# A second chunk of 128 tokens gathers its U rows, the dense U products become 256 wide, and more of them run ahead of the expert loop

## The chip, the cores and the metric

The kernel runs on one core of one Trainium2 chip. The metric is the device time of one execution in microseconds (us). A core has five engines with queues of their own: TensorE (PE in the profile; its weight loads are PEld), VectorE (DVE), ScalarE (ACT), GpSimd (POOL) and SyncE (SP), and 16 DMA engines which all of them feed. Here SP issues most loads, ACT most stores, and POOL the gathers, in which each partition fetches a row of its own.

## What is computed

One layer of an encoder on 512 tokens of width 1024: a layer norm, a projection, neighbourhood attention and latent attention, an output projection and a second layer norm; all of that is ahead of the part that changes. Then comes a feed-forward part with 16,384 experts, in which every token uses 128 (8 heads with 16 each):

```python
s1 = einsum('thd,kd->thk', q[..., :half], sub_keys[0]);  s2 = ...   # 128 keys each
v1, i1 = top_k(s1, 16);  v2, i2 = top_k(s2, 16)
cv, ci = top_k(v1[..., :, None] + v2[..., None, :], 16)              # over the 256 pairs
idx = e1 * 128 + e2                                                  # 128 experts a token
g = softmax(cv)
act = g * gelu(einsum('td,ted->te', xb, u_table[idx]))
out = einsum('te,ted->td', act, v_table[idx])
```

A sigmoid gate on a second input is added, and a last layer norm ends it.

## The kernel before

**Two ways to the experts.** Tokens come in four chunks of 128. For chunk 0 (`N_G = 128` tokens) the kernel gathers, for each of a token's 128 experts, the row of U and the row of V (4 KB each): one gather fetches 128 rows, one per token, 512 KB. VectorE multiplies such a tile with the tokens and sums along it (`gather_u`, line 1140), or adds it, scaled, to `base[0]` (`gather_v`, line 1149). For the other 384 tokens (`N_D`) the second product is dense: a matrix G, 16,384 experts by 384 tokens, holds each token's softmax weights and zeros elsewhere; it is built by one-hot products and kept in DRAM (`g_dram`, 24 parts of 16 tokens, 1 MB each). Experts come in 128 blocks of 128. The loop (line 1205) takes a block of G, multiplies it with the block's activations where these were computed densely, cuts it and the block's V rows into a high and a low part, and PE adds three products for each pair (`mm3`, line 103; `expert_out`, line 1163) into six PSUM banks, `acc`. That is 18 products 512 wide a block.

**The activations.** Of those 384 tokens the first `N_S = 96`, all in chunk 1, gather their U rows too: `own_rows` (line 885) fetches rows and multiplies them on VectorE with copies of the tokens (`h_s`), and the result is multiplied into the softmax weights `gws` before G is built from them. 96 tokens with 128 experts don't fill 128 partitions evenly, so the tokens are taken as groups of 64 and 32 (`S_PARTS`), and their index and result tables are moved between layouts by six small DMAs each way (`slices`, lines 892 to 911). There are 96 gathers. The last `N_U = 288` tokens get their activations densely, from products of each U block with all 288 tokens. `LEAD = 73` of the 128 blocks are done ahead of the loop, as plain f32 products (`lead_block`, line 942: 8 matmuls 288 wide, no cutting). The other 55 are done in the loop with `mm3` (`expert_in`, line 630): 24 products 288 wide, after ACT and VectorE have cut the block (`split`, line 86). The first `SPILL = 56` of the blocks ahead are stored to DRAM (`ge_dram`) and come back in the last part of the loop (line 1231).

**The stages around the change.** After the scores (lines 693 to 716) come, in an order written by hand for all engines (lines 1074 to 1100): `route` for chunk 1 (which experts, which weights), then `route` and `build_g` for chunk 2, the same for chunk 3, `route` for chunk 0, and last `build_g` for chunk 1, whose weights have to wait for its own rows. `run` (line 1056) goes through their steps. Each step yields an estimate of its VectorE time; `run` puts PE work beside it, `PACE = 1.1` us for each estimated us, taken from `gate_and_leads` (line 1012): the gate's products and the U blocks. With a share given (`OWN = 0.98`), it also puts in steps of `own_rows`, so many us of rows for one us of other steps. Nothing of `own_rows` is left for the last build. What PE work is left after it stands in the passage to the loop (lines 1183 to 1201), between the last product of G, the first load of G from DRAM (on POOL's queue, line 1187) and the first cut of V.

**Gathers of chunk 0.** They are 128 steps with U, one activation, and 128 with V. `PRE = 14` steps are done in the passage; the loop spreads the others by a formula (lines 1247 to 1252): an iteration counts 1 while U blocks are left in it, and `LATE = 0.5` after that, so that gathers run dense in the first part and half as dense in the second. They end some six iterations before the loop. `GATS = 8` buffers let POOL run ahead of VectorE.

Of the kernel before, what the change touches and what calls it, by code (L numbers as in the profile page):

```python
# [9 lines left out]
F32 = mybir.dt.float32  # L10
# [9 lines left out]
D = 1024  # L20
# [22 lines left out]
PRE = 14  # L43
OWN = 0.98
OWN_LATE = 10.0
# [8 lines left out]
NO_GATHER = 1  # L54
GE_AHEAD = 12
LOW = -3.0e38
FEED_NA = 2.75
# [8 lines left out]
def tile_encoder_layer(ctx: ExitStack, tc: tile.TileContext, A: dict, out: bass.AP):  # L66
# [559 lines left out]
    g_sel = pB.tile([128, NGC, 128], F32, name="g_sel")  # L626
    i_sel = pB.tile([128, NGC, 128], I32, name="i_sel")
    ge_t = {}

    def expert_in(i):  # L630

        ps = psH.tile([128, 512], F32, name="hp")
        u = stream(A["uT"][i], [8, 128])
        for k in range(8):
            mm3(ps[:, :N_U], (u[0][:, k], u[1][:, k]), (hTh[:, k, ts], hTl[:, k, ts]), k == 0, k == 7)
        ge = pB.tile([128, N_U], F32, name="ge", bufs=LEAD - SPILL + 1)
        nc.scalar.activation(ge, ps[:, :N_U], AF.Gelu)
        if i < SPILL:
            nc.sync.dma_start(ge_dram[i], ge)
        else:  # L640
            ge_t[i] = ge
# [174 lines left out]
    def build_g(c, e1, e2, gw, first):  # L816
# [64 lines left out]
        leave(ahead[0], sums)  # L881

    def own_rows(e1, e2, gw):
        ix = rg.tile([N_S, 128], I32, name="s_ix")
        nc.vector.scalar_tensor_tensor(ix, e1[0:N_S], 128.0, e2[0:N_S], op0=OP.mult, op1=OP.add)
        sel = rg.tile([128, N_S], I32, name="s_sel")
        dots = rg.tile([128, N_S], F32, name="s_dot")
        act = rg.tile([N_S, 128], F32, name="s_act")  # L890

        def slices():

            for lo, hi in S_PARTS:
                n = hi - lo
                for j in range(128 // n):
                    yield (slice(j * n, (j + 1) * n), slice(lo, hi)), (slice(lo, hi), slice(j * n, (j + 1) * n))

        for there, here in slices():
            nc.gpsimd.dma_start(sel[there], ix[here])  # L900
        yield 0.4
        for (lo, hi), x in zip(S_PARTS, h_s):
            for k in range(lo, hi):
                u = wst.tile([128, D], F32, name=("whi", "wlo")[k % 2])
                nc.gpsimd.indirect_dma_start(out=u[:], out_offset=None, in_=u_rows,
                                             in_offset=bass.IndirectOffsetOnAxis(ap=sel[:, k:k + 1], axis=0))
                nc.vector.scalar_tensor_tensor(u, u, 1.0, x, op0=OP.mult, op1=OP.mult, accum_out=dots[:, k:k + 1])
                yield 1.17
# [4 lines left out]
        nc.vector.tensor_tensor(gw[0:N_S], gw[0:N_S], act, op=OP.mult)  # L913

# [17 lines left out]
    def leave_u(i, ps):  # L932
        ge = pB.tile([128, N_U], F32, name="ge", bufs=LEAD - SPILL + 1)
# [140 lines left out]
    with tc.manual_schedule(engines={nc.vector.engine, nc.scalar.engine, nc.tensor.engine, nc.sync.engine,  # L1074
# [23 lines left out]
        run(lead0)  # L1098
        run(build)
        pb.close()  # L1100
# [29 lines left out]
    acc = [[psA.tile([128, 512], F32, name=f"acc{c}{hf}") for hf in range(2)] for c in range(NDC)]  # L1130
    hdot = pG.tile([128, NGC, 128], F32, name="hdot")
    scr = pG.tile([128, D], F32, name="scr")
# [70 lines left out]
    with tc.manual_schedule(engines={nc.vector.engine, nc.sync.engine}):  # L1203
        expert_in(LEAD)
        for n, i in enumerate(order):
# [23 lines left out]
            if 0 <= n + GE_AHEAD - (128 - SPILL) < SPILL:  # L1229
                ge = pB.tile([128, N_U], F32, name="ge", bufs=LEAD - SPILL + 1)  # L1230
                nc.sync.dma_start(ge, ge_dram[order[n + GE_AHEAD]])
# [126 lines left out]
```

## Time and profile before

| what | us |
|---|---|
| median of 3 runs | 1576.03 |
| lowest and highest | 1575.24, 1579.82 |
| the profiled execution, its own time | 1581.24 |
| its span | 1579.5 |

The profiled execution is a single run, 5.2 us above the median. In the profile an idle time is put down to what ended it; `<-` in a group stands between what an instruction writes and what it reads; "x128" is a count. An f32 matmul leaves two records each on PE. Records of matmuls overlap, since they are pipelined, so a matmul's cost is read from the distance between starts and not from a record's length.

| group of instructions | count | busy us |
|---|---|---|
| DVE products of chunk 0's U rows (L1142) | 128 | 156.6 |
| DVE sums of chunk 0's V rows (L1153) | 128 | 163.9 |
| PE records of U blocks ahead of the loop (L952, in `mm` and `hp`) | 624 and 544 | 157.5 and 137.1 |
| DVE cuts of 128x1024 blocks, U's among them (L90, `wlo`) | 134 | 157.1 |

### The profile page before, as it was taken

What the parts mean: (1) busy time and instruction counts of PE and PEld (TensorE: products, weight loads), DVE (VectorE), ACT (ScalarE), POOL (GpSimd) and SP (SyncE); (2) the same over time, 40 slices, a digit from 0 to 9 for tenths busy, and PEclk for the clock granted to TensorE, in tenths of its full rate; (3) what the DMA queues carried; (4) which work ended last, traced back from release to release, by engine and by line L of the source; (5) the groups of instructions that cost most, each with busy time, mean ns of one, the idle gap of its engine ahead of it and who ended that gap; (6) DMA issues with size and microseconds to landing.
All of it is one profiled execution on the core that took longest, in us unless ns stands there. A gap on an engine that the chain in (4) does not pass through costs nothing.

```text
span 1579.5 us, 23341 instructions
## 1 busy us (share of the span) xinstructions
PE 1526.9 (97%) x7963; PEld 1276.7 (81%) x7963; DVE 1311.7 (83%) x2990; ACT 689.9 (44%) x1266; POOL 498.1 (32%) x495
## 2 busy tenths in 40 slices
PE   6999999999999999999998899999999999999997
PEld 4788777788877788788786788989989878788885
DVE  7376685779989899888994799989889889799997
ACT  3365675333224682475472343433434333333333
POOL 1023000020015233432105455545545544344410
PEclk9999999999999999999999999999999999999999
DMA  7243231153269999999669999999999999999972
GB/s 230 63 117 90 75 121 41 60 157 91 91 211 313 345 371 362 351 414 385 238 238 383 371 376 375 388 366 361 378 369 345 357 360 381 388 380 387 386 290 80
DMA packets 204583, 437.73 MB, mean 277 GB/s; under 512 B 16784, under 2 KB 110384, under 8 KB 201392
## 3 DMA queue, kind: packets, MB, share of 16 engines
q1 hardware_dynamic: 138608, 210.79, 38.7%
q0 software_dynamic: 53984, 191.97, 32.6%
q10 hardware_dynamic: 11872, 33.48, 5.5%
q8 instruction: 63, 1.03, 0.3%
q14 instruction: 56, 0.46, 0.1%
HBM read 395.05 MB, written 37.62 MB: 274 GB/s over the span
## 4 chain that ended last, share of the span: by engine, by line
PE 71%; DMA 11%; DVE 10%; issue 4%; ACT 2%; SPq 1%; POOL 1%; DVEq 0%; POOLq 0%; ACTq 0%
PE acc L104 8%; PE acc L106 8%; PE acc L105 8%; PE mm L952 5%; PE hp L952 4%; DMA v_raw<-in_v_rows_dram 4%; PE tr L836 4%; PE hp L104 4%; PE hp L106 3%; PE hp L105 3%; PE mm L104 3%; PE mm L105 3%; PE mm L106 3%; PE pj L104 3%; PE pj L105 3%
## 5 line engine op out<-in xcount | busy, mean ns | idle before, releaser
L1151 POOL DMA_INDIRECT gat<-in_v_rows_dram,i_sel x128 | 169.9, 1328 | 203.2 <-DVE base L1153 178.6
L1136 POOL DMA_INDIRECT gat<-in_u_rows_dram,i_sel x128 | 171.1, 1337 | 183.5 <-DVE scr L1142 124.4
L104 PE MATMUL acc<-v_hi,a_hi 128*128 128x512 f32 x552 | 216.8, 393 | 4.4 <-ACT a_hi L89 4.4
L106 PE MATMUL acc<-v_hi,a_lo 128*128 128x512 f32 x552 | 216.8, 394 | 0.1
L105 PE MATMUL acc<-v_lo,a_hi 128*128 128x512 f32 x552 | 216.2, 392 | 0.0
L90 DVE TENSOR_TENSOR wlo<-raw,whi 128x1024 fp32r<-128x1024 f32 (+3 forms) x134 | 157.1, 1172 | 70.7 <-ACT whi L89 70.2
L89 ACT CAST whi<-raw 128x1024 fp32r<-128x1024 f32 (+3 forms) x134 | 135.1, 1008 | 145.3 <-PE mm L105 39.9
L89 ACT CAST v_hi<-v_raw 128x1024 fp32r<-128x1024 f32 x92 | 96.6, 1050 | 207.7 <-issue 126.8
L1153 DVE SCALAR_TENSOR_TENSOR base<-gat,hdot,base 128x1024 f32<-128x1024 f32 x128 | 163.9, 1281 | 1.7
L1142 DVE SCALAR_TENSOR_TENSOR scr<-gat,h 128x1024 f32<-128x1024 f32 x128 | 156.6, 1223 | 2.9
L952 PE MATMUL mm<-whole,raw 128*128 128x288 f32 x624 | 157.5, 407 | 1.2 <-DMA raw<-in_uT_dram 0.8
L952 PE MATMUL hp<-whole,raw 128*128 128x288 f32 x544 | 137.1, 407 | 5.4 <-DMA raw<-in_uT_dram 5.4
L952 PEld LDWEIGHTS mm<-whole,raw 128*128 128x128 f32 x624 | 116.0, 190 | 31.0 <-ACT ge L934 1.2
L89 ACT CAST a_hi<-gt 128x384 fp32r<-128x384 f32 x126 | 64.6, 513 | 174.8 <-DVE gt L1236 123.6
L90 DVE TENSOR_TENSOR v_lo<-v_raw,v_hi 128x1024 fp32r<-128x1024 f32 x92 | 112.6, 1224 | 28.0 <-ACT v_hi L89 27.8
L104 PE MATMUL hp<-hTh,whi 128*128 128x288 f32 x440 | 130.3, 296 | 1.0 <-ACT ge L934 1.0
L106 PE MATMUL hp<-hTh,wlo 128*128 128x288 f32 x440 | 130.1, 296 | 0.4 <-DVE wlo L90 0.4
L105 PE MATMUL hp<-hTl,whi 128*128 128x288 f32 x440 | 129.9, 295 | 0.0
L952 PEld LDWEIGHTS hp<-whole,raw 128*128 128x128 f32 x544 | 102.3, 190 | 33.0 <-issue 6.2
L104 PEld LDWEIGHTS acc<-v_hi,a_hi 128*128 128x128 f32 x552 | 104.2, 189 | 25.4 <-ACT a_hi L89 5.1
L106 PEld LDWEIGHTS acc<-v_hi,a_lo 128*128 128x128 f32 x552 | 104.1, 189 | 24.0 <-DVE a_lo L90 1.3
L105 PEld LDWEIGHTS acc<-v_lo,a_hi 128*128 128x128 f32 x552 | 104.3, 189 | 21.0 <-DVE v_lo L90 0.7
(353 smaller groups left out, 3383.0 us busy)
## 6 DMA issues: line engine op xcount, KB each, us to landing
raw<-in_uT_dram SPq DMA_DIRECT2D x128, 512.0 KB, 7.0
v_raw<-in_v_rows_dram SPq DMA_DIRECT2D x94, 512.0 KB, 9.5
g_dram<-g_st ACTq DMA_DIRECT2D x24, 1024.0 KB, 8.0
gt<-g_dram SPq DMA_DIRECT2D x15, 1536.0 KB, 15.1
raw<-in_v_rows_dram SPq DMA_DIRECT2D x34, 512.0 KB, 11.1
raw<-in_w_in_dram SPq DMA_DIRECT2D x17, 512.0 KB, 3.9
raw<-in_w_q_dram SPq DMA_DIRECT2D x16, 512.0 KB, 3.8
ge_dram<-ge ACTq DMA_DIRECT2D x56, 144.0 KB, 6.4
```

What stands on the lines that cost most here:

```text
L89: nc.scalar.copy(hi, src)
L90: nc.vector.tensor_tensor(lo, src, r32(hi), op=OP.subtract)
L104: nc.tensor.matmul(ps, a[0], b[0], start=start, stop=False)
L105: nc.tensor.matmul(ps, a[0], b[1], start=False, stop=False)
L106: nc.tensor.matmul(ps, a[1], b[0], start=False, stop=stop)
L836: nc.tensor.matmul(ps[:, i * 128:(i + 1) * 128], oj[:, 4 * r + i, :], oi[:, 4 * r + i, :], start=True, stop=True)
L952: nc.tensor.matmul(ps[:, :N_U], raw[:, k], whole[:, k, :], start=(k == 0), stop=(k == 7))
L1136: nc.gpsimd.indirect_dma_start(out=u[:], out_offset=None, in_=u_rows, in_offset=bass.IndirectOffsetOnAxis(ap=i_sel[:, c, k:k + 1], axis=0))
L1142: nc.vector.scalar_tensor_tensor(scr, u, 1.0, h[c], op0=OP.mult, op1=OP.mult, accum_out=hdot[:, c, k:k + 1])
L1151: nc.gpsimd.indirect_dma_start(out=u[:], out_offset=None, in_=v_rows, in_offset=bass.IndirectOffsetOnAxis(ap=i_sel[:, c, k:k + 1], axis=0))
L1153: nc.vector.scalar_tensor_tensor(base[c], u, hdot[:, c, k:k + 1], base[c], op0=OP.mult, op1=OP.add)
```

## The change

- `N_S` becomes 128: the whole of chunk 1 gathers its U rows, 128 gathers rather than 96. Tokens lie on partitions as in the tables, so the index and result tables need no other layout: the twelve small DMAs go, and one copy of the chunk (`h_s`) takes the place of two that hold it twice and four times.
- `N_U` becomes 256: all dense U products, ahead of the loop and in it, are 256 wide rather than 288.
- `LEAD` becomes 105 and `SPILL` 88: 105 blocks ahead of the loop and 23 in it; 88 blocks, now of 128 KB, go to DRAM and back. The buffers of `ge` are `GES = 20`, 18 before.
- Rows go into six buffers in turn (two each of `whi`, `wlo` and a new `row`), four before.
- `OWN` becomes 1.2, so that 128 rows fit beside the same steps.
- The first `BESIDE = 24` U rows of chunk 0 are fetched and multiplied beside the last build of G, with a share `OWN_G = 0.65`. `hdot`, which takes their results, is allocated earlier for that.
- `PRE` becomes 42: 24 of these steps beside the last build, and 18 in the passage, where there were 14.

```diff
-N_S = 96
-S_PARTS = ((0, 64), (64, 96))
+N_S = 128
-LEAD = 73
-SPILL = 56
+LEAD = 105
+SPILL = 88
-PRE = 14
-OWN = 0.98
+PRE = 42
+BESIDE = 24
+OWN = 1.2
+OWN_G = 0.65
+GES = 20
...
+    hdot = pB.tile([128, NGC, 128], F32, name="hdot")
...
-        ge = pB.tile([128, N_U], F32, name="ge", bufs=LEAD - SPILL + 1)
+        ge = pB.tile([128, N_U], F32, name="ge", bufs=GES)
...
-    h_s = [rw.tile([128, D], F32, name=f"h_s{lo}") for lo, hi in S_PARTS]
+    h_s = rw.tile([128, D], F32, name="h_s")
...
-            for (lo, hi), x in zip(S_PARTS, h_s):
-                for j in range(0, 128, hi - lo):
-                    nc.sync.dma_start(x[j:j + hi - lo, :], h[NGC][lo:hi, :])
+            nc.sync.dma_start(h_s, h[NGC])
...
+    def rows(ix, x, dots, ks):
+
+        for k in ks:
+            u = (rg if k % 3 == 2 else wst).tile([128, D], F32, name=("whi", "wlo", "row")[k % 3], bufs=2)
+            nc.gpsimd.indirect_dma_start(out=u[:], out_offset=None, in_=u_rows,
+                                         in_offset=bass.IndirectOffsetOnAxis(ap=ix[:, k:k + 1], axis=0))
+            nc.vector.scalar_tensor_tensor(u, u, 1.0, x, op0=OP.mult, op1=OP.mult, accum_out=dots[:, k:k + 1])
+            yield 1.17
 
     def own_rows(e1, e2, gw):
-        ix = rg.tile([N_S, 128], I32, name="s_ix")
-        nc.vector.scalar_tensor_tensor(ix, e1[0:N_S], 128.0, e2[0:N_S], op0=OP.mult, op1=OP.add)
-        sel = rg.tile([128, N_S], I32, name="s_sel")
...
-        for there, here in slices():
-            nc.gpsimd.dma_start(sel[there], ix[here])
+        ix = rg.tile([128, 128], I32, name="s_ix")
+        nc.vector.scalar_tensor_tensor(ix, e1, 128.0, e2, op0=OP.mult, op1=OP.add)
+        dots = rg.tile([128, 128], F32, name="s_dot")
         yield 0.4
-        for (lo, hi), x in zip(S_PARTS, h_s):
-            for k in range(lo, hi):
...
+        yield from rows(ix, h_s, dots, range(128))
         nc.scalar.activation(dots, dots, AF.Gelu)
-        for there, here in slices():
-            nc.scalar.dma_start(act[here], dots[there])
         yield 0.0
-        nc.vector.tensor_tensor(gw[0:N_S], gw[0:N_S], act, op=OP.mult)
+        nc.vector.tensor_tensor(gw, gw, dots, op=OP.mult)
...
-        run(build)
+        own = rows(i_sel[:, 0, :], h[0], hdot[:, 0, :], range(BESIDE))
+        own_due = 0.0
+        run(build, OWN_G)
+        for x in own:
+            run_pe(x)
         pb.close()
...
-        rows = [fetch_u(0, k) for k in range(GATS - 1)]
+        some = [fetch_u(0, BESIDE + k) for k in range(GATS - 1)]
...
-            gather_u(0, u, rows[u])
+            gather_u(0, BESIDE + u, some[u])
...
-        for k in range(7, PRE):
+        for k in range(BESIDE + 7, PRE):
             gather_u(0, k)
```

More of the change, by code (lines that the diff above doesn't have):

```diff
@@ L881, in build_g @@
         leave(ahead[0], sums)
-    def own_rows(e1, e2, gw):
-        ix = rg.tile([N_S, 128], I32, name="s_ix")
-        nc.vector.scalar_tensor_tensor(ix, e1[0:N_S], 128.0, e2[0:N_S], op0=OP.mult, op1=OP.add)
-        sel = rg.tile([128, N_S], I32, name="s_sel")
[L889 to L897, printed above, removed]
-        for there, here in slices():
-            nc.gpsimd.dma_start(sel[there], ix[here])
-        yield 0.4
-        for (lo, hi), x in zip(S_PARTS, h_s):
-            for k in range(lo, hi):
[L904 to L908, printed above, removed]
+    def rows(ix, x, dots, ks):
[5 more added lines that the diff above has]
+            yield 1.17
+    def own_rows(e1, e2, gw):
+        ix = rg.tile([128, 128], I32, name="s_ix")
+        nc.vector.scalar_tensor_tensor(ix, e1, 128.0, e2, op0=OP.mult, op1=OP.add)
+        dots = rg.tile([128, 128], F32, name="s_dot")
+        yield 0.4
+        yield from rows(ix, h_s, dots, range(128))
         nc.scalar.activation(dots, dots, AF.Gelu)
-        for there, here in slices():
-            nc.scalar.dma_start(act[here], dots[there])
         yield 0.0
-        nc.vector.tensor_tensor(gw[0:N_S], gw[0:N_S], act, op=OP.mult)
+        nc.vector.tensor_tensor(gw, gw, dots, op=OP.mult)
     PRODUCT_U, PRODUCT_G = 0.49 * N_U / 288, 0.69
@@ L932, in leave_u @@
     def leave_u(i, ps):
-        ge = pB.tile([128, N_U], F32, name="ge", bufs=LEAD - SPILL + 1)
+        ge = pB.tile([128, N_U], F32, name="ge", bufs=GES)
         nc.scalar.activation(ge, ps[:, :N_U], AF.Gelu)
@@ L1229, in tile_encoder_layer @@
             if 0 <= n + GE_AHEAD - (128 - SPILL) < SPILL:
-                ge = pB.tile([128, N_U], F32, name="ge", bufs=LEAD - SPILL + 1)
+                ge = pB.tile([128, N_U], F32, name="ge", bufs=GES)
                 nc.sync.dma_start(ge, ge_dram[order[n + GE_AHEAD]])
```

1 line of the change is left out of this document (removed).

## The prediction, made before the changed kernel ran

> **What bounds the kernel now.** I read the page's shares and its slices first: which engine is full, and where.
>
> ```profile
> span 1579.5 us, 23341 instructions
> PE 1526.9 (97%) x7963; PEld 1276.7 (81%) x7963; DVE 1311.7 (83%) x2990; ACT 689.9 (44%) x1266; POOL 498.1 (32%) x495
> GB/s 230 63 117 90 75 121 41 60 157 91 91 211 313 345 371 362 351 414 385 238 238 383 371 376 375 388 366 361 378 369 345 357 360 381 388 380 387 386 290 80
> ```
>
> TensorE is busy nearly throughout, VectorE has little to spare, and from the thirteenth slice on the DMA engines move 340 to 414 GB/s with two gaps. Three resources are near their ends, so the shares decide nothing. I cut the span at the stages, where the timeline shows the transposes that open each build of G, the last product, and the end of the loop.
>
> ```profile
> core 0: us, PE busy (x) PEld busy (x) DVE busy (x) ACT busy (x) POOL busy (x), PEclk, DMA share, GB/s
> 421.00:494.50 73.50, 73.28 (x310) 57.76 (x309) 65.51 (x261) 17.36 (x29) 17.27 (x18) 1.00 0.65 215
> 494.50:649.70 155.20, 152.16 (x767) 124.17 (x765) 142.96 (x378) 82.48 (x190) 58.02 (x51) 1.00 0.97 357
> 649.70:769.00 119.30, 118.05 (x623) 98.30 (x622) 104.57 (x314) 71.83 (x171) 32.73 (x34) 1.00 0.91 351
> 769.00:825.00 56.00, 54.68 (x364) 48.38 (x363) 52.51 (x159) 42.08 (x103) 7.68 (x7) 1.00 0.72 263
> 825.00:858.00 33.00, 26.10 (x115) 19.93 (x113) 12.68 (x19) 7.23 (x12) 14.43 (x14) 1.00 0.97 357
> 858.00:1259.00 401.00, 396.61 (x2255) 355.64 (x2256) 356.92 (x487) 157.21 (x219) 212.80 (x153) 0.99 1.00 369
> 1259.00:1505.00 246.00, 245.45 (x1068) 198.83 (x1067) 217.85 (x258) 87.52 (x119) 103.34 (x81) 1.00 1.05 379
> 1505.00:1558.00 53.00, 53.00 (x231) 42.72 (x230) 44.80 (x63) 19.86 (x27) 4.96 (x4) 1.00 0.57 219
> ```
>
> Rows two to four are the three builds of G with the routing between them; the fifth is the passage to the loop; then the loop with U blocks, without them, and its end without gathers. Busy matmuls overlap in the records, so I check whether PE really runs without gaps by the distance between starts, in one iteration of the loop:
>
> ```profile
> 866.09 0.39 PE L104 MATMUL acc<-v_hi,a_hi 128*128 128x512 f32 x1
> 870.20 0.30 PE L104 MATMUL hp<-hTh,whi 128*128 128x288 f32 x1
> 873.41 0.39 PE L104 MATMUL acc<-v_hi,a_hi 128*128 128x512 f32 x1
> ```
>
> 18 products of 512 columns in 4.11 us, 24 of 288 in 3.21 us: 7.32 us. 54 such iterations are 395 of the sixth row's 401 us, and the 73 others at 4.11 us are 300 of the last two rows' 299. **The loop goes at PE's pace.** The build stages nearly do: PE waits there for hardly anything, VectorE chiefly for gathered rows.
>
> ```profile
> DVE whi L907 <- DMA whi<-in_u_rows_dram,s_sel: 13.6, 13, 2.1
> DVE wlo L907 <- DMA wlo<-in_u_rows_dram,s_sel: 8.2, 10, 1.6
> PE hp L952 <- DMA raw<-in_uT_dram: 5.4, 2, 3.8
> ```
>
> So an edit is worth what it takes from PE, as long as VectorE and the DMA engines can follow.
>
> **The change, part by part.** *The U products on PE.* The chain of waits has unbroken runs of the products ahead of the loop (plain f32, two records a matmul), and of G's 128 wide f32 products:
>
> ```profile
> 423.49 26.21 PE hp L952 x108
> 532.75 1.78 PE tr L836 x16
> ```
>
> 26.21/108 = 0.2427 us a record at 288 columns, 1.78/16 = 0.1113 at 128. A block is 8 matmuls, 16 records: 3.883 us. No f32 product 256 wide is in the trace; between those two rows a straight line gives 0.1113 + 0.1314 x 128/160 = 0.2164, 3.463 us a block. Its bounds are the plain ratio 256/288 (3.452) and no gain at all (3.883); two widths of one kind bracket it, so I take 3.463. In the loop the line between 3.21/24 = 0.1338 at 288 and 4.11/18 = 0.2283 at 512, carried to 256, gives 0.1203: 2.887 us a block, at most 3.21.
>
> - Ahead of the loop: 105 x 3.463 - 73 x 3.883 = 363.6 - 283.5 = **+80.1 us**.
> - In the loop: 23 x 2.887 - 55 x 3.21 = 66.4 - 176.6 = **-110.2 us**.
> - Net on PE: **-30.1 us**, if every wait that PE has now stays as it is.
>
> By the issue order of the two programs, PE reaches the three builds after 14, 38.25 and 61 blocks before, and 16.6, 48.25 and 80.4 after, and the end of the last after 67.4 and 95.9. The first build comes 8 us of PE later (16.6 blocks and 96 gate products at 0.2283 against 14 and 75); the three build stages then grow by 10.6, 23 and 29 us, the passage by 9.7.
>
> *The passage.* Before, it is this:
>
> ```profile
> 824.91 10.35 PE L952 MATMUL hp<-whole,raw 128*128 128x288 f32 x42
> 836.87 4.12 PE L952 MATMUL hp<-whole,raw 128*128 128x288 f32 x16 [1.61 <-DMA raw<-in_uT_dram]
> 844.77 8.00 PE L952 MATMUL hp<-whole,raw 128*128 128x288 f32 x32 [3.78 <-DMA raw<-in_uT_dram]
> 858.24 0.50 PE L104 MATMUL acc<-v_hi,a_hi 128*128 128x512 f32 x1 [0.36 <-ACT a_hi L89]
> ```
>
> 90 records at 0.2427 and a U block of 3.21 are 25.0 us of work in 33.3: 8.3 us lost while G's last part goes to DRAM and comes back. After, 9.1 blocks and one of 2.887 are 34.5 us, which would cover the loss; but 18 rather than 14 gathered rows stand there beside more U loads on DMA engines that already make PE wait. Between 0 and -8.3 I take 0, since the two waits named are for loads.
>
> *VectorE.* A row costs this:
>
> ```profile
> L907 DVE SCALAR_TENSOR_TENSOR whi<-whi,h_s x48: 1206/1216/1268, 473.9 to 744.3; 128x1024 f32<-128x1024 f32 x48
> L1142 DVE SCALAR_TENSOR_TENSOR scr<-gat,h 128x1024 f32<-128x1024 f32 x128 | 156.6, 1223 | 2.9
> L90 DVE TENSOR_TENSOR wlo<-raw,whi 128x1024 fp32r<-128x1024 f32 (+3 forms) x134 | 157.1, 1172 | 70.7 <-ACT whi L89 70.2
> ```
>
> 32 more of the second chunk's rows and 24 of the first chunk's moved up are 56 x 1.22 = 68.3 us ahead of the loop, 4.9 of it ahead of the first build. In the three build stages VectorE is busy 300.0 of 330.5 us; after, 363.4 us, about 6 us of small waits, and the waits for rows. PE has 330.5 + 62.6 = 393 us there. Rows wait 21.8/96 = 0.227 us each now; at that price 152 rows wait 34.5 us, VectorE needs 404 and ends 11 us after PE; with six buffers in turn rather than four a row may land later unseen, and below 0.155 us a row nothing shows. I take the middle, **+6**. In the loop VectorE loses 28 gathers and 32 cuts of U, 28 x 1.22 + 32 x 1.17 = 72 of 619.6 us (the last three stage rows): 548 of some 590, room enough.
>
> *DMA.* Sizes by the page's issues:
>
> ```profile
> raw<-in_uT_dram SPq DMA_DIRECT2D x128, 512.0 KB, 7.0
> v_raw<-in_v_rows_dram SPq DMA_DIRECT2D x94, 512.0 KB, 9.5
> gt<-g_dram SPq DMA_DIRECT2D x15, 1536.0 KB, 15.1
> ge_dram<-ge ACTq DMA_DIRECT2D x56, 144.0 KB, 6.4
> gat<-in_v_rows_dram,i_sel POOLq DMA_INDIRECT x128, 8.1
> ```
>
> 32 gathers of 512 KB are +16.8 MB; 88 spilled blocks of 128 KB for 56 of 144 KB, written and read, +6.6 MB. A late iteration moves 0.524 (V) + 0.197 (G) + 0.131 (ge) + 1.50 rows of 0.524 = 1.64 MB in 4.11 us: 399 GB/s. An iteration with a U block moves 0.524 more and 3.0 rows, 2.82 MB in 7.0 us: 403 GB/s. (The rows per iteration are those of the loop's own formula.) The late loop holds 379 GB/s now, in slices up to 388. At 388 a late iteration takes 4.22 us and an early one 7.26: 11 us over 100 iterations and 6 over 23. Gathers run eight buffers ahead, 4.2 MB or 11 us of transfer, and a lag up to that is paid from stock: between 0 and 17 I take 17 - 11 = **+6**.
>
> *What costs nothing.*
>
> ```profile
> 455.38 2.88 DMA s_sel<-s_ix
> PE tr L822 <- DVE gws L913: 0.9, 1, 0.9
> L1151 POOL DMA_INDIRECT gat<-in_v_rows_dram,i_sel x128 | 169.9, 1328 | 203.2 <-DVE base L1153 178.6
> ```
>
> The six index copies on POOL's queue go, and the six of the activated products on ACT's. The first took 2.88 us of the chain ahead of the first row, where PE has its own stock of blocks to work through; the second delayed PE by no more than 0.9 us. The 32 more ge loads on SP, ahead of V loads in its queue, come one an iteration, as 56 do now while PE is busy 245.45 of 246 us. POOL at 32% has room for 32 more issues of 1.3 us; the load of G's first part stands behind the 24 rows on its queue, but waits for the last product anyway.
>
> **Sum:** -30.1 + 6 + 6 = -18.1 us. The profiled execution took 1581.24 us (1579.5 and what lies around the span), so 1563.1; it stood 5.2 above the median of the runs shown, 1576.03, to which the forecast is made: **1558 us**.
>
> **The rivals.** *The DMA engines become the bound* (slower). From 494.5 to 1505 us the stage rows give 365.0 MB in 1010.5 us, 361 GB/s. After it is 16.8 + 6.6 more, less 1.7 for blocks ahead of that stretch: 386.7 MB. The forecast leaves 1010.5 - 18 - 8 = 984.5 us, 393 GB/s on average, without the gap that 263 GB/s shows in the last build. If no more than the long late stretch's 379 is held, it takes 1020 us: +9.8, and 8 us ahead of it, 1594 us. It decides below 386.7/1002.5 = 386 GB/s. For it: 379 is the best of any long stretch, and VectorE already waits for rows at 357. Against it: PE lost nothing at 379, so that was demand and not the limit, and slices reach 414.
>
> The Trainium skill's HBM Reference (section Specifications (TRN2)) gives about 358 GB/s for each core and about 425 for a core that streams alone, bound by its 16 DMA engines. By the first, those 386.7 MB would take 1080 us, which speaks against the change, 1654 us in all; by the second there is room. The trace holds 369 and 379 over hundreds of us, above the first, and slices of 414, below the second; the measured rates decide.
>
> *Rows come late in the builds* (no change). If a row waits 0.30 us rather than 0.227, VectorE needs 369.4 + 152 x 0.30 = 415 us where PE needs 393: +22, with 6 in the loop 1574 us. The late one-hots hold up G's products, and so the loop. For it: a build stage asks 61 rows, 31.6 blocks and G in 166 us, some 390 GB/s, against 357 now. Against: two more buffers.
>
> *Nothing is late*: the passage's loss is covered and no friction shows: -30.1 - 8.3, 1538 us.
>
> *The narrow product is no shorter* (the change doesn't do what it says on PE): 105 x 3.883 + 23 x 3.21 - 460.1 = +21.4, 1597 us. The 128 wide row speaks against it.
>
> **How the numbers follow.** Forecast 0.55, nothing late 0.10; rows late 0.15; DMA bound 0.16; no shorter product 0.04. So faster 0.65, same 0.15, slower 0.20, with 0.3% (4.7 us) as what a measurement can tell from no change. The range goes from 1538 to 1592: it leaves out the last rival, half of the DMA rival, which reaches beyond its 1594, and little below. The forecast with its side "nothing late" alone holds 1538 to 1570.
>
> **What would show it.** Right: f32 products at 0.216 us a record and U blocks of 2.9 us in the loop; a first acc product some 80 us later and a loop some 105 us shorter; PE without gaps at 4.1 us an iteration; 390 GB/s or more from the first build on. Wrong: VectorE's waits for rows above 45 us in the builds; PE waiting for a_hi or a_lo late in the loop because gathers stand ahead on VectorE; landing times of V and the rows well above 8 to 11 us; late iterations of 4.2 us and more.

## The result, and the profile after

| | before | after |
|---|---|---|
| median of 20 runs, us | 1575.77 | 1588.59 |
| lowest and highest, us | 1572.43, 1584.31 | 1579.25, 1594.39 |
| the profiled execution, us | 1581.24 | 1590.2 |
| its span, us | 1579.5 | 1588.0 |

The ratio of the times is 1.0071, with a 95% interval of 1.0057 to 1.0085: the change makes the kernel **slower by 0.7%**. The forecast was 1558, 18 us less than before; the time moved 12.8 us the other way. It lies in the range, near the 1594 of the rival in which the DMA engines become the bound.

These are the lines of the page after that answer to those of before: the shares, the clock and the transfers by slices.

```profile
span 1588.0 us, 22850 instructions
PE 1512.1 (95%) x7707; PEld 1267.7 (80%) x7707; DVE 1302.6 (82%) x3022; ACT 655.5 (41%) x1234; POOL 563.1 (35%) x521
PEclk9999999999999999999999989999999999999999
GB/s 229 63 117 94 70 120 41 72 137 88 103 241 355 319 390 405 413 415 418 416 310 411 342 403 380 382 401 354 366 365 358 357 381 384 384 383 384 361 305 80
```

PE is busy 14.8 us less in a span 8.5 us longer, so PE waits more. The slices of the builds carry up to 418 GB/s, those of the loop 354 to 401 as long as it gathers. The stages, cut at the same places as before (the three builds, the passage, the loop with U blocks, without them, its end):

```profile
core 0: us, PE busy (x) PEld busy (x) DVE busy (x) ACT busy (x) POOL busy (x), PEclk, DMA share, GB/s
502.50:673.80 171.30, 164.36 (x863) 143.49 (x862) 151.75 (x395) 82.52 (x193) 68.55 (x63) 0.99 0.99 381
673.80:818.30 144.50, 141.22 (x777) 126.60 (x776) 126.07 (x350) 75.57 (x181) 47.62 (x51) 1.00 0.98 391
818.30:901.80 83.50, 82.56 (x506) 75.49 (x505) 78.61 (x200) 46.79 (x111) 31.85 (x28) 1.00 1.00 394
901.80:948.80 47.00, 39.57 (x174) 33.83 (x174) 23.27 (x37) 8.75 (x17) 24.75 (x21) 0.90 0.98 369
948.80:1112.00 163.20, 157.05 (x925) 139.09 (x924) 142.28 (x212) 59.60 (x85) 83.21 (x64) 0.98 1.02 380
1112.00:1520.00 408.00, 390.93 (x1664) 310.94 (x1663) 353.73 (x442) 138.09 (x189) 232.25 (x140) 1.00 1.03 372
1520.00:1577.00 57.00, 56.54 (x245) 45.06 (x244) 47.82 (x80) 22.76 (x33) 4.40 (x3) 1.00 0.45 168
```

Set against the forecast, stage by stage (the stages of before are those that the prediction shows; its loop ran from 858.2 to 1569.3 us, 711.1):

| stage | before | forecast | after | after less forecast |
|---|---|---|---|---|
| up to the first build | 494.6 | 502.6 | 502.5 | -0.1 |
| three builds | 330.2 | 398.8 | 399.3 | +0.5 |
| passage | 33.4 | 43.1 | 47.0 | +3.9 |
| loop | 711.1 | 606.9 | 628.8 | **+21.9** |

Ahead of the loop the forecast holds. In the loop it fails: PE's saving of 110 us came out as 82. The waits of PE in the loop say where; first after, then before (total us, times, longest):

```profile
PE acc L106 <- ACT a_hi L91: 23.5, 16, 3.1
```

```profile
PE acc L104 <- ACT a_hi L89: 4.9, 3, 4.0
```

After the last U block, 17.4 of those 23.5 us fall on 14 waits, against one wait of 0.5 us before. They come about once for each load of G, every 35 us. One of them, on SP's queue, then ACT, then PE:

```profile
1119.91 0.38 SPq L1103 DMA_DIRECT2D gt<-g_dram  x1
1120.39 5.60 SPq L1113 DMA_DIRECT2D v_raw<-in_v_rows_dram  x1
```

```profile
1123.98 1.05 ACT L91 CAST v_hi<-v_raw 128x1024 fp32r<-128x1024 f32 x1 [1.04 <-issue]
1127.51 0.52 ACT L91 CAST a_hi<-gt 128x384 fp32r<-128x384 f32 x1 [2.47 <-DVE gt L1228]
1133.37 1.04 ACT L91 CAST v_hi<-v_raw 128x1024 fp32r<-128x1024 f32 x1 [5.35 <-DMA v_raw<-in_v_rows_dram]
1134.32 0.51 ACT L91 CAST a_hi<-gt 128x384 fp32r<-128x384 f32 x1
```

```profile
1132.66 0.39 PE L108 MATMUL acc<-whi,a_lo 128*128 128x512 f32 x1
1134.88 0.50 PE L106 MATMUL acc<-v_hi,a_hi 128*128 128x512 f32 x1 [1.83 <-ACT a_hi L91]
```

A load of G goes out, and the V load behind it takes 5.6 us on SP's queue. ACT then stands 5.35 us waiting for V rows, and the cut of `a`, which needs no V, stands behind that in its queue. PE waits for `a`. Among VectorE's waits late in the loop none is for a gathered tile: the gathers were never late there.

The place itself is not new. In the kernel before, SP's queue shows the same:

```profile
1296.73 0.38 SPq L1110 DMA_DIRECT2D gt<-g_dram  x1
1297.15 7.38 SPq L1120 DMA_DIRECT2D v_raw<-in_v_rows_dram  x1
```

After the last U block the V load behind a load of G took 5.8 to 9.5 us there before, 5.0 to 7.4 after. As far as their landings are on record (68 of 68 V loads before, 50 of 100 after), the V rows don't land later either: the median is 11.3 us before and 10.8 after, the longest 17.5 and 17.8. What is new is that PE has to wait there.

### The profile page after: what moved, and what is told of

Read it like the earlier page. It is cut to its first block, busy times and chain, and to the rows that moved or that the text cites. A ratio compares the mean times of both kernels' runs of the same rounds, so it can differ in the third digit from the quotient of the medians.

```text
span 1588.0 us, 22850 instructions
## 1 busy us (share of the span) xinstructions
PE 1512.1 (95%) x7707; PEld 1267.7 (80%) x7707; DVE 1302.6 (82%) x3022; ACT 655.5 (41%) x1234; POOL 563.1 (35%) x521
## 4 chain that ended last, share of the span: by engine, by line
PE 52%; DMA 20%; DVE 15%; issue 6%; SPq 3%; ACT 2%; POOL 1%; ACTq 0%; DVEq 0%; POOLq 0%
PE mm L941 10%; DMA v_raw<-in_v_rows_dram 5%; DMA raw<-in_uT_dram 5%; DMA raw<-in_v_rows_dram 5%; PE hp L941 4%; PE tr L837 4%; PE mm L106 3%; PE mm L108 3%; PE mm L107 3%; PE pj L106 3%; PE pj L107 3%; PE pj L108 3%; PE acc L106 3%; PE acc L107 3%; PE acc L108 3%
## 5 line engine op out<-in xcount | busy, mean ns | idle before, releaser
L941 PE MATMUL mm<-whole,raw 128*128 128x256 f32 x1088 | 244.6, 380 | 5.7 <-DMA raw<-in_uT_dram 5.5
L941 PEld LDWEIGHTS mm<-whole,raw 128*128 128x128 f32 x1088 | 202.5, 190 | 35.7 <-ACT ge L923 6.6
L106 PE MATMUL acc<-v_hi,a_hi 128*128 128x512 f32 x456 | 180.0, 396 | 10.2 <-ACT a_hi L91 10.2
L91 ACT CAST whi<-raw 128x1024 fp32r<-128x1024 f32 (+4 forms) x118 | 118.2, 1002 | 149.9 <-PE mm L107 39.9
L92 DVE TENSOR_TENSOR wlo<-raw,whi 128x1024 fp32r<-128x1024 f32 (+4 forms) x118 | 136.8, 1159 | 36.0 <-ACT whi L91 35.5
L941 PE MATMUL hp<-whole,raw 128*128 128x256 f32 x592 | 136.0, 386 | 8.1 <-DMA raw<-in_uT_dram 7.1
L106 PE MATMUL acc<-whi,a_hi 128*128 128x512 f32 x300 | 120.2, 401 | 13.3 <-ACT a_hi L91 13.3
L92 DVE TENSOR_TENSOR a_lo<-gt,a_hi 128x384 fp32r<-128x384 f32 x126 | 69.6, 552 | 66.2 <-ACT a_hi L91 64.0
L108 PE MATMUL acc<-whi,a_lo 128*128 128x512 f32 x300 | 120.4, 401 | 0.0
L107 PE MATMUL acc<-wlo,a_hi 128*128 128x512 f32 x300 | 119.0, 397 | 0.0
L871 DVE TENSOR_SCALAR oh_j<-iota,eT 128x128 f32<-128x128 f32 x384 | 116.5, 376 | 0.0
## 6 DMA issues: line engine op xcount, KB each, us to landing
ge<-ge_dram SPq DMA_DIRECT2D x88, 128.0 KB, 10.5
```

Source lines behind the costliest of these rows:

```text
L91: nc.scalar.copy(hi, src)
L92: nc.vector.tensor_tensor(lo, src, r32(hi), op=OP.subtract)
L106: nc.tensor.matmul(ps, a[0], b[0], start=start, stop=False)
L107: nc.tensor.matmul(ps, a[0], b[1], start=False, stop=False)
L108: nc.tensor.matmul(ps, a[1], b[0], start=False, stop=stop)
L871: nc.vector.tensor_scalar(oj[:, i], iota, eT[:, 1, t0 + i:t0 + i + 1], eT[:, 2, t0 + i:t0 + i + 1], op0=OP.is_equal, op1=OP.mult)
```

## The experiments

Each ratio is to the kernel before, in runs on the same chip. "Late" is the time from the last U product to the last `acc` product (106 iterations here: 1908 products, 18 an iteration; 465.7 us after), read from one profile each. The changed kernel itself ran only for the result, with executions from 1579 to 1594 us, and the edited ones later, on four chips, so a difference of a few us between two rows is not safe.

| run | median us | ratio, 95% interval | late us | PE waits there |
|---|---|---|---|---|
| after | 1588.59 | 1.0071 (1.0057 to 1.0085) | 465.7 | 17.4 |
| a fourth of V's gathers left out | 1569.73 | 0.9932 (0.9910 to 0.9954) | 447.8 | 4.7 |
| VectorE adds half of a row | 1579.87 | 1.0001 (0.9982 to 1.0020) | 460.9 | 12.7 |
| no reload of spilled blocks | 1583.53 | 1.0007 (0.9979 to 1.0035) | 462.0 | 14.2 |
| G's load in three parts | 1575.89 | 0.9989 (0.9962 to 1.0016) | 462.0 | 14.2 |
| G's load from ACT's queue | 1612.30 | 1.0201 (1.0163 to 1.0239) | 483.1 | 29.5 |
| one V buffer more | 1582.73 | 1.0013 (0.9993 to 1.0033) | 468.0 | 16.0 |
| ACT's order | 1579.93 | 0.9992 (0.9976 to 1.0009) | 455.6 | 6.7 |
| order, parts | 1574.55 | 0.9965 (0.9952 to 0.9978) | 449.8 | 3.8 |
| order, parts, no reload | 1563.29 | 0.9916 (0.9890 to 0.9941) | 439.3 | 0.0 |
| order, parts, spread | 1571.32 | 0.9960 (0.9945 to 0.9975) | 443.6 | 1.8 |
| the same, 31 steps ahead | 1574.38 | 0.9989 (0.9974 to 1.0003) | 455.8 | 7.4 |

Runs with another number of blocks ahead, or built on the kernel before, are told further below.

### Bytes, VectorE or SP: four runs

A fourth of V's gathers left out (VectorE takes the row before instead):

```diff
+        if k % 4 == 3:
+            u = held_v[0]
+        else:
+            u = pG.tile([128, D], F32, name="gat", bufs=GATS)
+            nc.gpsimd.indirect_dma_start(out=u[:], ...)
+            held_v[0] = u
```

> The changed kernel with every fourth of chunk 0's 128 V gathers left out: VectorE still adds a tile, the one fetched last, so those 32 of chunk 0's sums use a wrong row. VectorE, PE and the SP queue keep all their work; 16.8 MB of transfers go, nearly all from the part of the loop without U blocks. In the changed kernel that part (end of the last U product to the end of the last acc product) takes 465.6 us for 105 iterations, 4.43 each, against 4.23 for 73 before. Theory D (the DMA engines' time sets that part): 16.8 MB at 380 GB/s are 44 us, of which PE's own pace lets through 105 x 0.20 = 21: some 445 us there, 1568 us in all. Theory V (VectorE's order sets it): nothing changes, 466 and 1588. Theory S (V loads are issued late, because SP stands still behind each load of G): 460 to 466, 1583 to 1588.

VectorE adds only half of each of chunk 0's V rows, so the output of those tokens is incomplete:

```diff
-        nc.vector.scalar_tensor_tensor(base[c], u, hdot[:, c, k:k + 1], base[c], ...)
+        nc.vector.scalar_tensor_tensor(base[c][:, 0:512], u[:, 0:512], hdot[:, c, k:k + 1], base[c][:, 0:512], ...)
```

> The changed kernel with VectorE adding only the first 512 of 1024 columns of each gathered V row of chunk 0, so half of that sum is left out: some 0.6 us of VectorE less for each of 128 rows, 77 us in all, with every transfer as it was. V: the part without U blocks falls from 466 to some 445 us, 1568 in all. D: within 4 us of 466, 1585 to 1590. S: the same as D.

One spilled block is loaded and used for all 88:

```diff
+                if not ge_held:
                     ge = pB.tile([128, N_U], F32, name="ge", bufs=GES)
                     nc.sync.dma_start(ge, ge_dram[order[n + GE_AHEAD]])
+                    ge_held.append(ge)
+                ge = ge_held[0]
```

> The changed kernel with one reload of spilled activations in place of 88: the 88 blocks are all multiplied with the first one's, which is wrong for 87. 87 x 128 KB = 11.4 MB of transfers and 87 issues on SP's queue go; VectorE and PE keep their work. D: 11.4 MB at 380 GB/s are 30 us, of which PE's pace lets 21 through: 445 us in the part without U blocks, 1568 in all. V: nothing. S: some of SP's stand still goes as well, 455 to 466, 1578 to 1588.

The later loads of G in three parts of 512 KB, one an iteration:

```diff
-            if n % GB == GB // 2 and n + GB // 2 < 128:
-                gt_next = load_g(n + GB // 2)
+            if n % GB >= GB // 2 and n + GB // 2 < 128 and n % GB < GB // 2 + 3:
+                gt_next = load_part(n)
```

> The changed kernel with each later load of G (1536 KB) issued in three parts of 512 KB in three iterations that follow one another, so that SP is not held for 6.7 us at a time behind it and the V loads go out sooner; bytes and packet sizes are the same. S: V lands in time, 450 us or less in the part without U blocks, 1573 or less in all. D and V: within 4 us of 466, 1585 to 1590.

Fewer gathers gave what the DMA theory said, 447.8 us. Half of VectorE's sums gave 5 us where VectorE's theory asked for 21, so VectorE is not the main cause; the total, 1579.87, met no theory's range. But the reload left out, 11.4 MB, gave 4 us where the same DMA theory asked for some 20. The 350 us from 1150 suggest why; first after, then without the reload:

```profile
1150.00:1500.00 350.00, 337.13 (x1441) 269.61 (x1440) 302.95 (x370) 118.53 (x162) 201.80 (x119) 1.00 1.03 375
```

```profile
1150.00:1500.00 350.00, 342.01 (x1472) 274.58 (x1471) 307.85 (x376) 122.12 (x165) 208.80 (x122) 1.00 0.97 347
```

With less to move, the engines moved less: they pause while PE waits, since no buffer comes free. Between 1130 and 1500 us SP stood 175.2 us with a V load that waited for VectorE's cuts to free a buffer, 32.3 after. A mean rate is no limit where the transfers pause. G's load in parts brought the total to that of before, but PE's waits late in the loop stayed at 14.2 us. The early part was 8.5 us shorter in that profile, 154.6 us; that proves little, since with the same loads in parts it took 168.2 us in a profile further below, and between 152.7 and 168.5 in the profiles of kernels without that edit.

### V's lateness: queue, buffers, or the order on ACT

The later loads of G from ACT's queue:

```diff
-                gt_next = load_g(n + GB // 2)
+                gt_next = load_g(n + GB // 2, nc.scalar)
```

> One queue changed: the later loads of G (1.5 MB, one in eight iterations) are issued by ACT instead of SP, so that the next V load no longer stands behind them in SP's queue. Theory Q (after the first four runs: the loop loses its time where a V load is issued some 6.7 us late and then lands late, once per G load, not by the mean rate of the DMA engines): the late waits of ACT for v_raw and PE's stall of 0.5 to 2 us per G load go, the loop (628.8 us after) comes down to 604 to 612, the time to 1565 to 1573. Theory D (mean rate of the DMA engines): the same bytes, so nothing changes, 1588 within 4. Rival: ACT itself stands still for some 6 us at each issue, and its cuts come late: PE stalls as often as now or more, 1585 to 1600.

It got worse, 1612 us. ACT waited less for V rows, 74.1 us from 1116 us on where it was 116.5, but in single waits of up to 12.9 us, and PE waited more, 29.5 us for `a_hi` in seven waits, and 24.3 us for loads of U in the passage. ACT's issues of G take 0.37 us each, so the rival in which ACT stands still is not it. SP stood still instead, longer than before the edit; these are its waits from 1113 to 1500 us:

```profile
SPq L1113 <- DMA gt<-g_dram: 135.6, 8, 21.1
```

The profile puts eight waits ahead of V loads, of up to 21.1 us, down to the landing of G's load. So this edit sent V loads out later and not sooner, and the run can't tell whether theory Q holds. What speaks against Q as the whole cause is the run with G's load in parts, which left 14.2 us of waits.

One buffer more for V, one less for gathers:

```diff
-GATS = 8
+GATS = 7
...
-pV.tile([128, D], F32, name="v_raw", bufs=3)
+pV.tile([128, D], F32, name="v_raw", bufs=4)
```

> The changed kernel with one more buffer for V's rows (four v_raw) and one less for gathers (seven). V loads are issued up to two iterations earlier in the late loop, where even blocks use these buffers. Theory A: half of the late loads get that time, PE's waits late fall by some half, 1575 to 1582. Theory D: the same bytes, 1588 within 4, or a little more with the smaller stock of gathers.

The time is about where the upper end of theory A (late V loads cost time only through ACT's order, told below) put it, but late nothing changed, 468.0 us with 16.0 of waits; in that profile the gain lies in the early part (157.0 us), which varies by as much. It tells little.

ACT's order is the scheduler's choice here; only VectorE's and SP's are the program's own. The instructions of ACT around the first cut from a new group of G, which is cut `a` for a block n divisible by 8, stand so after (left) and as the program is written (right):

```
v_hi   V of block n               whi    V of block n - 1
a_hi   a of block n - 1           a_hi   a of block n - 1
whi    V of block n + 1           v_hi   V of block n
a_hi   a of block n, new G        a_hi   a of block n, new G
```

The scheduler has V a block ahead all along the late loop, in the kernel before as well; the V load behind a load of G is that of the block four before such an n. So I made ACT's order the program's own in the last 105 iterations:

```diff
-    with tc.manual_schedule(engines={nc.vector.engine, nc.sync.engine}):
-        expert_in(LEAD)
-        for n, i in enumerate(order):
+    def blocks():
+        own = {nc.vector.engine, nc.sync.engine}
+        todo = list(enumerate(order))
+        with tc.manual_schedule(engines=own):
+            expert_in(LEAD)
+            yield from todo[:128 - LEAD]
+        with tc.manual_schedule(engines=own | {nc.scalar.engine}):
+            yield from todo[128 - LEAD:]
+    for n, i in blocks():
```

> The changed kernel, with ACT's order in the loop's last 105 iterations as the program is written: the cut of V for block n, then the cut of a for block n. As changed, the cut of V for block n + 1 stands ahead of the cut of a for block n in ACT's queue, so a V load that lands late holds back a product that doesn't need it. Theory A (late V loads cost time only through this order): they get one iteration, 4.1 us, more; PE's 17.4 us of waits late in the loop fall to 4 or less, the late part from 466 to 438 to 446, the time to 1560 to 1568. Theory D (mean rate of the DMA engines): the same bytes in the same time, 1588 within 4. Rival: the cut of V no longer runs ahead, VectorE stands waiting for it in each iteration with the gathers' sums behind it: 1588 to 1600.

The waits fell as theory A said, nearly; these are PE's from 1115 us on in that run:

```profile
PE acc L106 <- ACT a_hi L91: 5.6, 3, 4.2
PE acc L107 <- DVE v_lo L92: 1.1, 3, 0.4
```

The time gained 8.7 us by the medians, not the 20 to 28 that A asked for: late it is 10.1 us shorter, at 455.6. The order is a cause, and not the only one. With G's load in parts as well:

> Both: ACT's order as in the run above, and each later load of G in three parts of 512 KB over three iterations. The parts alone gave 1575.9 with the early loop 8.5 us shorter and 14.2 us of waits late. Theory A: those waits go too, 1553 to 1562, faster than both kernels. Theory D: nothing on top, 1572 to 1579.

Late 449.8, 15.9 us less than after; yet the time is 12.6 us above the upper end that A gave, and where theory D put it.

### What is left: the mean rate

Both edits, and the reload left out, so that 11.4 MB less are read:

> ACT's order and G's load in parts, and one block of spilled activations loaded and used for all 88, so 11.4 MB less are read and the results are not the reference's. Alone, with the old order, this gave 5 us, with pauses of the DMA engines left. D2: 1.51 MB an iteration need 3.95 us at 383 GB/s, less than PE's 4.2: the late part 440 to 444, 1563 to 1569. Rival P: 1571 to 1576.

Both edits, and gathers that end 2.5 steps of their formula later:

```diff
-            upto = min(len(steps), PRE + math.ceil((len(steps) - PRE) * spent / (128 - (1 - LATE) * LEAD - 3 - NO_GATHER)))
+            upto = min(len(steps), PRE + math.ceil((len(steps) - PRE) * spent / (128 - (1 - LATE) * LEAD - 0.5 - NO_GATHER)))
```

> The run with ACT's order and G's load in parts (1574.6 us; late in the loop the DMA engines never pause, 383 GB/s, 4.28 us an iteration), with the loop's gathers ending 2.5 steps of their formula later: 3.4% fewer rows to each iteration. Theory D2 (with the pauses gone, the mean rate of the DMA engines sets the late pace, 1.64 MB at 383 GB/s): 1.59 MB, 4.15 us, so PE's own 4.2 us sets it: 441 to 445 for the late part, 1564 to 1570 in all. Rival P (PE and the cuts set 4.28, whatever the bytes): 1573 to 1577.

The same 350 us with both edits; with both and no reload; with both and spread:

```profile
1150.00:1500.00 350.00, 346.25 (x1477) 275.59 (x1476) 309.12 (x375) 122.93 (x165) 192.93 (x123) 1.00 1.05 383
```

```profile
1150.00:1500.00 350.00, 350.00 (x1522) 285.43 (x1521) 322.13 (x385) 125.02 (x171) 209.37 (x125) 1.00 1.00 365
```

```profile
1150.00:1500.00 350.00, 348.20 (x1503) 281.38 (x1502) 311.58 (x378) 124.51 (x169) 199.74 (x121) 1.00 1.05 383
```

With order and parts alone the engines carry 383 GB/s over the whole stretch; 1.64 MB an iteration at that rate are 4.28 us, and 1477 products, 18 an iteration, in 350 us are 4.27. With 11.4 MB less, PE has no wait and the rate falls to 365 GB/s: 1522 products, 4.14 us an iteration, PE's own pace, and 439.3 us late. The same edit that gave 4 us beside the pauses gives 10.5 without them. That edit also takes 87 issues from SP's queue; spread takes none and points the same way. It gives 443.6, as D2 said; the total of 1571.3 misses its 1570 by little, since the end after the last product grew from 10.0 to 14.0 us. So D2 (the mean rate sets the late pace) holds and rival P falls: **this mix gets 383 GB/s over a long stretch, and PE's pace asks for 3% more**, 1.64 MB in 4.14 us. It is a mean: slices of 20 us reach 400 GB/s in the profile of after.

The rows behind G's first load moved from the passage into the loop:

```diff
-PRE = 42
+PRE = 31
```

> As the run above, with 31 rather than 42 of chunk 0's steps ahead of the loop: the 11 whose gathers stand behind G's first load on POOL's queue leave the passage. D2: the passage gets 8 to 10 us shorter, but 5.8 MB more go through the DMA engines in the loop, 15 us at 383 GB/s, of which the room that the spread gave takes some; 3 to 8 us slower than the run above. If the DMA engines have room in the loop: 8 to 10 us faster than it.

3.1 us slower than with 42, as D2 said: late was 12.2 us longer. The passage took 41.5 rather than 45.3 us, a gain of 3.8 where 8 to 10 had been expected.

### Other numbers of blocks ahead, and the kernel before

Two runs of the changed kernel with fewer blocks ahead (the second with 73 and 56), and one of the kernel before with the blocks of after:

```diff
-LEAD = 105
-SPILL = 88
+LEAD = 97
+SPILL = 80
```

> 97 blocks ahead and 80 spilled rather than 105 and 88; all else as changed. On PE: 8 x (3.463 - 2.887) = 4.6 us less; 2.1 MB less go through the DMA engines, and the gathers of the loop come 1.40 rather than 1.47 rows to a late iteration, 0.04 MB less of 1.64. Theory D: a late iteration then needs 1.60 MB, 4.1 us at 390 GB/s, so the loop's loss goes almost whole: 1560 to 1568. Theory Q: the stall at each G load stays, 10 of 12, 1578 to 1584.

1589.36 us, ratio 1.0060 (1.0031 to 1.0090): both theories missed. Late, an iteration took 4.32 us, 4.39 after (422.9/98, 465.7/106). But the passage had no stock of blocks left: PE waited there 12.1 us, and 14.1 more in the early part, at a mean clock of 0.77 and 0.94. The blocks ahead also cover the passage, which neither theory counted.

> The width and the rows alone: 73 blocks ahead and 56 spilled, as before; 256 wide products, 128 gathered rows and the 24 rows beside the last build as changed. PE has 73 x 3.463 and 55 x 2.887 us of U products, 49 us less than before, but the builds have only some 53 blocks to put beside VectorE's 363 us and its waits for rows, so VectorE sets them: some 395 us where 330 were. The loop has 55 early iterations of 7.0 and 73 late ones of 4.13 us, some 687 rather than 711, and 1.2 gathered rows to a late iteration. Both D and Q: 1612 to 1625, with no stall late in the loop by D and small ones by Q.

1617.68 us, ratio 1.0232 (1.0196 to 1.0268), as expected: the width and the rows alone make the kernel slower. In the builds PE waited for VectorE, and in the loop, at 1.2 rows an iteration and 319 GB/s, it waited for nothing late and took 4.14 us an iteration.

> The kernel before with 105 blocks ahead and 88 spilled alone; 288 wide products and 96 gathered rows as before. PE: 32 x (3.883 - 3.21) = 21.5 us more. In the loop the 114 U and 128 V gathers left are spread over 23 early iterations instead of 55: 1.65 rows to a late iteration, 1.74 MB, 4.5 us at 388 GB/s. If the DMA engines' mean rate sets the loop (D): 1600 plus some 25 to 35, 1625 to 1635. By Q: 1600 plus 1.5 to 2 us for each of 12 G loads, 1615 to 1624. If nothing is late: 1597 to 1601.

1690.40 us, ratio 1.0684 (1.0644 to 1.0723), much more than any theory gave. The builds and the passage grew by 123.3 us, which is the forecast's price, 32 x 3.883; early took 164.4; but the 106 late iterations took 537.5, 5.1 each, with 69.9 us of waits and a clock of 0.92. So the more the gathers ask, the longer PE waits late: 69.9 us here at 1.65 rows an iteration, 17.4 after at 1.47, 10.2 with 97 blocks ahead at 1.40, none with 73 at 1.2. It isn't the rows alone: the kernel before, with some 1.4 by the loop's formula, had 0.5 us.

ACT's order in the kernel before, and then all three edits in it:

> The kernel before with ACT's order in its last 73 iterations as the program is written. PE waits there for 0.5 us in all, so by each theory next to nothing is to be had: the same as before within 4 us. If it gains 8 us or more, the order costs something that the waits do not show.

> The kernel before with all three edits (ACT's order late, G's load in parts, gathers that end later). PE waited there for 0.5 us late, and the order alone gave 3.6 us, so 1570 to 1576 by every theory; if so, and the changed kernel with the same edits takes 1564 to 1570, the change itself is worth some 6 us with them.

1575.71 us, ratio 0.9972 (0.9959 to 0.9985), and 1575.54, 0.9970 (0.9953 to 0.9987), both within what was expected. So the changed kernel with the three edits, 0.9960 (0.9945 to 0.9975), beats both kernels, but the kernel before with the same edits stands 4.2 us from it by the medians and 1.6 by the ratios, and the intervals overlap: how much the change is worth then, if anything, isn't settled.

## Why the prediction was wrong

**The U products: right.** These 48 records give 0.219 us each where 0.216 was forecast, with the modelled end of the last in it.

```profile
902.39 10.52 PE L941 MATMUL hp<-whole,raw 128*128 128x256 f32 x48
```

In the loop a block takes 2.83 us from its first product's start to that of the next `acc` product (1006.79 to 1009.62), forecast 2.887.

**The builds: right in the sum, not in its parts.** Rows waited far less than the 34.5 us reckoned, 14.0 us over 152 rows. The columns are total us, times, longest:

```profile
DVE row L890 <- DMA row<-in_u_rows_dram,s_ix: 4.5, 6, 1.9
DVE wlo L890 <- DMA wlo<-in_u_rows_dram,s_ix: 4.1, 5, 1.5
DVE whi L890 <- DMA whi<-in_u_rows_dram,s_ix: 3.9, 4, 2.0
DVE wlo L890 <- DMA wlo<-in_u_rows_dram,i_sel: 1.0, 1, 1.0
DVE whi L890 <- DMA whi<-in_u_rows_dram,i_sel: 0.5, 1, 0.5
```

The two more buffers may have done that, no run tells; 391 and 394 GB/s were held. The stages still came out 0.5 us above the forecast; among what took the place is one wait of 4.5 us for U at 509 us and the clock that fell after it.

**The passage: 3.9 us short.** The forecast saw that G's first load stands behind the 24 rows on POOL's queue, and not that 11 more rows stand behind that load:

```profile
885.54 1.69 POOL L1128 DMA_INDIRECT gat<-in_u_rows_dram,i_sel  x1 [0.30 <-issue]
903.48 1.24 POOL L1103 DMA_DIRECT2D gt<-g_dram  x1 [16.26 <-ACT ge L923]
912.62 0.90 POOL L1103 DMA_DIRECT2D gt<-g_dram  x1 [7.91 <-issue]
913.83 1.01 POOL L1128 DMA_INDIRECT gat<-in_u_rows_dram,i_sel  x1 [0.30 <-issue]
925.88 1.23 DVE L1134 SCALAR_TENSOR_TENSOR scr<-gat,h 128x1024 f32<-128x1024 f32 x1 [1.30 <-DMA gat<-in_u_rows_dram,i_sel]
```

No gather is issued from 887 to 914 us, and VectorE's rows then come at the pace at which they land. In the run with 31 steps ahead, which leaves these 11 rows out of the passage, it was 3.8 us shorter.

**DMA in the loop: the step that failed.** The forecast allowed a lag of 17 us and had 11 paid "from stock", as gathers run eight buffers ahead; it took +6. The loop lost 27.9. Two things were wrong in it. First, the stock is one of gathers, and what PE waited for stood behind V: the gathers were never late. A stock in one queue didn't pay for a lag in another. That the deep stock itself holds the V loads back is not shown: V landed no later than before, as far as it is on record, and the run with one buffer of gathers fewer, and one of V more, gained nothing late. Second, "PE lost nothing at 379, so that was demand and not the limit" left out how near the limit was: with the pauses gone the loop's mix holds 383, 1% more.

Of the 27.9 us, 26.4 are late, the 465.7 us against the 439.3 at which PE has no wait; 1.5 are left for the early part, less than its profiles differ. Step by step, the late part shrinks by 10.1 us with V's place ahead of `a` in ACT's queue put right (to 455.6), by 5.8 with G's load in parts (to 449.8) and by 10.5 with fewer bytes (to 439.3; the spread recovers 6.2 of them). These shares are rough, from one execution each: that of ACT's order was the slowest of its ten, that of order and parts the slowest of its six, that without the reload the fastest of its four. By the ratios the steps are some 12, 4 and 8 us. The 5.8 of G's load in one piece is the least certain, since from 1150 to 1500 us order alone ran 1490 products and order with parts 1477.

A slip in the forecast's count changes little: it had 54 iterations with a U block and 73 without, 127 in all; the products say 74 without, and 106 after.

**The rival in which the DMA engines become the bound** had its arithmetic met: the stage rows from 502.5 to 1520 give 385.8 MB in 1017.5 us, 379 GB/s, where it said 1020 us at 379. That its 1594 came so near is in part luck. The rate alone, with the pauses gone, is some 10 of the 27.9 us; most of the rest is pauses, in which, by the account above, a late V load stops PE, and so the release of buffers, and so the transfers. That both come of asking for about as much as the engines carry fits PE's late waits, which in the changed kernel grow with the rows an iteration gathers; it isn't tested by itself. The rows late in the builds did not come, and the narrow product is shorter.

With order, parts and spread the profiled execution takes 1568.58 us, 5.5 above the 1563.1 that the forecast gave for a profiled one; the median, 1571.32, is 13 above its 1558. With the late part at PE's own pace, the account of PE was sound, and that of the queues was not.

## What to carry to other kernels

Near the DMA engines' limit, ask of each load that PE needs next how early it is issued and what else stands in front of it in the queues, SP's, the cutting engine's and the DMA engines'; a deep stock of other data in flight doesn't stand in for it. Before a rate is taken as the bound or as mere demand, look whether the transfers pause: here only the stretches without pauses showed the limit. A rate at which the busiest engine loses nothing says only that the limit isn't lower. And where a scheduler sets an engine's order, look whether an instruction that waits for a load stands ahead of one that needs none.

## What the runs showed of the hardware that had not been expected

**A wait of 2 to 4 us can cost PE more than itself.** After a wait of 3.07 us PE's next products start 0.43 us apart, eight of them, then 0.23 again:

```profile
976.79 0.28 PE L108 MATMUL hp<-hTh,wlo 128*128 128x256 f32 x1
980.14 0.73 PE L106 MATMUL acc<-v_hi,a_hi 128*128 128x512 f32 x1 [3.07 <-ACT a_hi L91]
981.94 0.63 PE L107 MATMUL acc<-v_lo,a_hi 128*128 128x512 f32 x1
982.37 0.63 PE L108 MATMUL acc<-v_hi,a_lo 128*128 128x512 f32 x1
983.65 0.40 PE L108 MATMUL acc<-v_hi,a_lo 128*128 128x512 f32 x1
983.89 0.40 PE L106 MATMUL acc<-v_hi,a_hi 128*128 128x512 f32 x1
```

In 4 us steps the granted clock falls to between 0.50 and 0.65 at six places after (near 508, 916, 944, 980, 1096 and 1488 us), and at one before (892). The mean clock is 0.987 of 1588.0 us after and 0.994 of 1579.5 before: 20.6 and 9.5 us of full clock not granted, 11 us between them, in waiting time and in work. The length of the wait alone doesn't decide it: waits of 2.6 us near 916 and 2.0 near 1488 came with such a fall, the 1.83 us wait shown above did not (products 0.23 to 0.34 us apart), and in the kernel before the wait of 3.78 us that ended at 844.77 did not either (granted clock 1.00 from 844 to 848). The Trainium skill (TensorE: Matmul & The Clock Gate, section "HAM oscillation — how this bites in real kernels") has the rule "no PE-idle gaps >~3.4µs", since the clock is halved after one. The traces agree only in part: here shorter waits came with half the clock, and one longer than that did not. The forecast priced waits at their length alone.

**The rate depends on the stage.** In the builds, slices of 40 us hold 413 to 418 GB/s one after another; late in the loop without pauses 383 is the most over 350 us, with G and spilled blocks among the loads. What lowers it wasn't tried.
